# One ring of seven eviction buffers, mask and rotary-key operand laid over it, rotary query rows first: a hybrid attention layer on one Trainium2 core

## The chip, the cores and the metric

The program runs on one core of a Trainium2 chip. The metric is the device time of one launch in microseconds (us); lower is better. Engines are named as the profile names them: PE (TensorE matmuls), PEld (its weight loads), DVE (VectorE), ACT (ScalarE), POOL (GpSimd) and SP (SyncE, which here only issues DMAs).

## The reference

One layer of a hybrid encoder over 1072 rows: 32 sample rows, 16 meta rows and 1024 prompt rows, with a cache of 512 older rows for the sample stream. Cut to what matters here:

```python
c_q, c_kv, k_r, f_q, f_k, f_v, f_logit = jnp.split(h @ w_in, IN_SPLIT_POINTS, axis=-1)
q = (rms_norm(c_q, q_norm) @ w_uq).reshape(B, L, MLA_HEADS, MLA_QK_DIM)
q_mla = jnp.concatenate([q[..., :MLA_NOPE], rope(q[..., MLA_NOPE:], pos)], axis=-1)
latent = rms_norm(c_kv, kv_norm)
k_rope = rope(k_r[:, :, None, :], pos)[:, :, 0, :]
kv = (latent @ w_ukv).reshape(B, K, MLA_HEADS, MLA_NOPE + MLA_V)   # MLA keys, values
o_a = attend(q_mla, k_mla, v_mla, MLA_SCALE, chunk mask)           # 8 heads
o_b = attend(f_q, f_k, f_v, FOX_SCALE, causal, fox_bias(cum, cum)) # 8 forgetting heads
x = x + jnp.concatenate([o_a, o_b], -1) @ w_out
h = rms_norm(x, norm_ffn)
return x + (jax.nn.silu(h @ w_gate) * (h @ w_up)) @ w_down
```

## The kernel before, in words

Every float32 operand of a product is kept as a rounded high part and a low part, and a product is three matmuls (high by high, high by low, low by high: `mm3`, lines 119 to 121). The function `split` makes the two parts: ACT copies the high one, DVE (or POOL for some weights) subtracts. `spill` and `spill_v` split a PSUM result into an eviction buffer in SBUF and send it to a scratch tensor in DRAM with a DMA that POOL issues (`put`, line 63). `load` and `move` are DMAs that SP issues (lines 57 and 60).

The program has three stages. The first normalizes the input and makes the projections (PE's lines 291 to 384). The second is attention, in two halves: heads 8 to 15 (forgetting) and then heads 0 to 7 (latent). `attention` walks the heads; `fetch` and `fetch_v` load the operands of the next head; `scores` multiplies (line 579), finds the row maximum on DVE (line 582) and takes the exponential on ACT (line 587); `values` transposes (lines 617, 641), splits and multiplies with the values (lines 627, 655 to 658). The third stage is the output projection's second half and the feed-forward network (line 805 on).

Between the pieces of attention a *filler* is stepped, so that PE has other products to do. For heads 8 to 15 the filler is `latent_heads(ev)`: 16 steps that make the latent keys (`w_uk`, four blocks by four column chunks, to `sK`), 26 steps that make the latent values (`w_uv`, line 485 on, to `sV`), and 18 steps that make the queries (`w_uq`, blocks m = 0 to 5 by three chunks; m 0 to 3 go to `sQ`, m 4 and 5 are the rotary rows and go to `sQR`). For heads 0 to 7 the filler is `out_half(ev)`: 24 half products of the output projection with a residual read from `xT` and a result sent to `sX2`. All filler products share one PSUM buffer, the tile `psF`.

The eviction buffers before: key and query steps use two tiles `es` of the pool `evq` and, every third step, a free part of the slot `A_lo` (function `es(n)`, lines 458 to 463). Value steps use two parts of the slot `A_hi` (`vts`, line 465). A rotary step loads its factors into the one tile `cs` (line 508), with the one temporary `et` and one `et2`. `out_half` has two tiles `xt`.

The tile `B3` holds three copies of the rotary keys and ten rows of masks. Heads 0 to 7 multiply with it in `scores`; its four moves (lines 764 to 767) stand in the code ahead of the first attention half.

The order on each engine is made by the framework from the code when the program is built; each engine then works strictly in that order. Buffers are guarded by semaphores: whoever writes a buffer waits for all who used it, so an eviction into a buffer waits until the DMA out of it has landed.

Of the kernel before, what the change touches and what calls it, by code (L numbers as in the profile page):

```python
# [9 lines left out]
F32 = mybir.dt.float32  # L10
# [30 lines left out]
FC = [(0, 408), (408, 408), (816, 256)]  # L41
LAG = 2
LN_EXP = "natural_log_exp_and_others"
OB = 112
# [4 lines left out]
def trunk(ctx: ExitStack, tc: tile.TileContext, a):  # L49
# [6 lines left out]
    def load(out, in_):  # L56
        sp.dma_start(out=out, in_=in_)
# [383 lines left out]

    def latent_heads(ev):

# [12 lines left out]
        turn = [0]  # L456

        def es(n):

            turn[0] += 1  # L460
            if turn[0] % 3 == 0:
                return lo[:, 3 * T:3 * T + 2 * n].rearrange("p (j t) -> p j t", j=2)
            return ev.tile([128, 2, 396], FR, tag="es", name="es")

        vts = [hi[:, 3 * T + 512 * j:3 * T + 512 * j + 512].rearrange("p (h d) -> p h d", h=4) for j in range(2)]
        todo = [("w_uk", m, 2, 128) for m in range(4)] + [("w_uv", m, 2, 256) for m in range(2)]
        ws = [weights(*todo[0])]
        yield
        for m in range(6):
            if m + 1 < 6:  # L470
                ws.append(weights(*todo[m + 1]))
            w = ws[m]
            if m < 4:
                for c0, n in KC:
                    ps = psF.tile([128, 512], F32, tag="psF", name="psF")
                    mm3(ps[:, :n], lambda k: w[0][:, k], lambda k: w[1][:, k],
                        lambda k: l_hi[:, k, c0:c0 + n], lambda k: l_lo[:, k, c0:c0 + n], 2)
                    spill(es, sK[m, :, :, c0:c0 + n], ps[:, :n], n)
                    yield
            else:  # L480
                for kt, (k0, n) in enumerate([(128 * i, 128) for i in range(4)] + [(PAST + t0, n) for t0, n in QT]):
                    ps = psF.tile([128, 512], F32, tag="psF", name="psF")
                    for k in range(2):
                        s_hi, s_lo = l_hi[:, k, k0:k0 + 128], l_lo[:, k, k0:k0 + 128]
                        pe.matmul(ps[:, :256], s_hi, w[0][:, k], start=(k == 0), stop=False)
                        pe.matmul(ps[:, :256], s_hi, w[1][:, k], start=False, stop=False)
                        pe.matmul(ps[:, :256], s_lo, w[0][:, k], start=False, stop=(k == 1))
                    spill_v(ev, k0, 4 * (m - 4), ps[:n, :256], n, vts[kt % 2])
                    yield
# [3 lines left out]
        move(c_lo, sCQ[:, :, 1].rearrange("k p t -> p k t"))  # L493
        ws = [weights("w_uq", 0, 3, 128)]
        yield
        for m in range(6):
            if m + 1 < 6:
                ws.append(weights("w_uq", m + 1, 3, 128))
            w = ws[m]
            for c0, n in CC:  # L500
                ps = psF.tile([128, 512], F32, tag="psF", name="psF")
# [4 lines left out]
                else:  # L506
                    cs = ev.tile([128, 2, 358], F32, tag="cs", name="cs", bufs=1)
                    load(cs[:, :, :n], a["trig"][:, :, c0:c0 + n])
                    t1 = ev.tile([128, 358], F32, tag="et", name="et", bufs=1)
                    act.activation(t1[:, :n], ps[:, :n], AF.Copy, scale=SCALE)  # L510
                    t2 = ev.tile([128, 358], F32, tag="et2", name="et2", bufs=1)
                    dve.stream_shuffle(t2[:, :n], t1[:, :n], [(i + 16) % 32 for i in range(32)])
                    dve.tensor_tensor(out=t2[:, :n], in0=t2[:, :n], in1=cs[:, 1, :n], op=ALU.mult)
                    dve.tensor_tensor(out=t1[:, :n], in0=t1[:, :n], in1=cs[:, 0, :n], op=ALU.mult)
                    dve.tensor_tensor(out=t1[:, :n], in0=t1[:, :n], in1=t2[:, :n], op=ALU.add)
                    spill(es, sQR[m - 4, :, :, c0:c0 + n], t1[:, :n], n)
                yield

# [9 lines left out]

    def out_half(ev):

        hi, lo = (rows4(t) for t in mixed["B"])
        out_weights(1)
        for m in range(8):
            out_weights(m + 2)
            w = w_ring[m]
            for c0, n in CC:
                xt = ev.tile([128, 358], F32, tag="xt", name="xt")
                load(xt[:, :n], a["xT"][128 * m:128 * m + 128, c0:c0 + n])
# [176 lines left out]
    def attention(hs, filler, steps, last):  # L715
# [11 lines left out]
        for h in hs:  # L727
# [4 lines left out]
            if h == hs[-1]:  # L732
                for _ in filler:
                    pass
            nops = fetch(nxt) if nxt in heads else None
            if h % 2 == 0:
# [26 lines left out]
    mixed["B"] = (slot("B_hi"), slot("B_lo"))  # L763
    B3 = st.tile([106, NK], FR, tag="B3", name="B3", bufs=1)
    for j, part in enumerate((0, 0, 1)):
        move(B3[32 * j:32 * j + 32], sKR[:, part])
    move(B3[96:106], sMK[0:10])
    mixed["B3"] = B3
    with tc.tile_pool(name="evq", bufs=2) as ev:
        attention(range(8, 16), latent_heads(ev), 62, False)  # L770
    mixed["A"] = (slot("A_hi"), slot("A_lo"))
    with tc.tile_pool(name="evo", bufs=2) as ev:

        attention(range(0, 8), out_half(ev), 48, True)
        for _ in state["pend"]:
            pass
    B.close()
# [282 lines left out]
```

## Time and profile before

| what | value |
|---|---|
| median of 3 runs | 1563.72 us (1559.86 to 1563.76) |
| the profiled execution's own time | 1564.27 us |
| span of its instructions | 1562.5 us |
| PE busy | 1502.2 us (96%) |
| DVE busy | 969.3 us (62%) |
| ACT busy | 594.3 us (38%) |
| POOL busy | 213.4 us (14%) |
| mean granted TensorE clock | 0.987 |
| first attention half, then second, in the trace | about 233 to 488 us, about 488 to 711 us |

The profiled execution lies 0.55 us above the median of the runs, and 1.8 us of its time lie outside the span. A share of busy time is an average over the three stages, so it does not say which engine sets the end in attention. Matmuls are pipelined and their ends are modelled in the trace, so PE counts as busy for a little while after it has stopped.

### The profile page before, as it was taken

What the parts mean: (1) busy time and instruction counts of PE and PEld (TensorE: products, weight loads), DVE (VectorE), ACT (ScalarE), POOL (GpSimd) and SP (SyncE); (2) the same over time, 40 slices, a digit from 0 to 9 for tenths busy, and PEclk for the clock granted to TensorE, in tenths of its full rate; (3) what the DMA queues carried; (4) which work ended last, traced back from release to release, by engine and by line L of the source; (5) the groups of instructions that cost most, each with busy time, mean ns of one, the idle gap of its engine ahead of it and who ended that gap; (6) DMA issues with size and microseconds to landing.
All of it is one profiled execution on the core that took longest, in us unless ns stands there. A gap on an engine that the chain in (4) does not pass through costs nothing.

```text
span 1562.5 us, 24281 instructions
## 1 busy us (share of the span) xinstructions
PE 1502.2 (96%) x9309; PEld 1440.7 (92%) x9309; DVE 969.3 (62%) x1853; ACT 594.3 (38%) x1204; POOL 213.4 (14%) x342
## 2 busy tenths in 40 slices
PE   9999998988998999999999999999999999999995
PEld 8999997877787988888999999999999999999995
DVE  7874616756767666775945556555555555555647
ACT  7453436655765665663611111111112111111124
POOL 0343241422232122210000000000000000000014
PEclk9999999999999999999999999999999999999998
DMA  5689557766867767625101111111111111111003
GB/s 193 234 256 307 168 199 214 254 176 183 234 202 194 198 163 181 161 70 193 55 28 41 61 54 49 42 41 41 41 41 41 47 63 54 41 41 41 28 1 113
DMA packets 88469, 185.28 MB, mean 119 GB/s; under 512 B 9819, under 2 KB 53787, under 8 KB 88261
## 3 DMA queue, kind: packets, MB, share of 16 engines
q1 hardware_dynamic: 71424, 129.44, 28.7%
q0 software_dynamic: 16928, 54.29, 9.9%
q8 instruction: 74, 1.21, 0.3%
q14 instruction: 43, 0.34, 0.1%
HBM read 125.02 MB, written 58.67 MB: 118 GB/s over the span
## 4 chain that ended last, share of the span: by engine, by line
PE 82%; DMA 5%; DVE 4%; ACT 4%; issue 3%; POOL 1%; SPq 0%; DVEq 0%; POOLq 0%; ACTq 0%
PE psG L120 11%; PE psG L119 11%; PE psG L121 11%; PE psD L873 5%; PE psD L874 5%; PE psD L872 5%; PE psS L579 4%; PE psA L121 3%; PE psA L119 3%; PE psA L120 3%; PE psT L641 3%; PE po L657 2%; DMA sV<-A_hi 2%; PE po L658 1%; DMA sK<-es 1%
## 5 line engine op out<-in xcount | busy, mean ns | idle before, releaser
L881 DVE TENSOR_TENSOR x<-psD,x 128x408 f32<-128x408 f32 (+1 forms) x496 | 236.3, 522 | 5.7 <-PE psD L874 5.7
L119 PE MATMUL psG<-B_hi,gh 128*128 128x408 f32 (+1 forms) x528 | 172.7, 327 | 0.0
L119 PE MATMUL psG<-A_hi,gh 128*128 128x408 f32 (+1 forms) x528 | 172.6, 327 | 0.0
L120 PE MATMUL psG<-A_lo,gh 128*128 128x408 f32 (+1 forms) x528 | 172.6, 327 | 0.0
L120 PE MATMUL psG<-B_lo,gh 128*128 128x408 f32 (+1 forms) x528 | 172.5, 327 | 0.0
L874 PE MATMUL psD<-ah,dl 128*128 128x408 f32 (+1 forms) x528 | 172.1, 326 | 0.0
L121 PE MATMUL psG<-B_hi,gl 128*128 128x408 f32 (+1 forms) x528 | 171.8, 325 | 0.0
L121 PE MATMUL psG<-A_hi,gl 128*128 128x408 f32 (+1 forms) x528 | 171.8, 325 | 0.0
L873 PE MATMUL psD<-al,dh 128*128 128x408 f32 (+1 forms) x528 | 171.7, 325 | 0.0
L872 PE MATMUL psD<-ah,dh 128*128 128x408 f32 (+1 forms) x528 | 170.9, 325 | 0.1
L861 ACT ACTIVATE sl<-sl 128x408 f32<-128x408 f32 (+1 forms) x66 | 33.1, 502 | 354.4 <-DVE sl L860 354.4
L865 DVE TENSOR_TENSOR sq<-psG,rb 128x408 f32<-128x408 f32 (+1 forms) x66 | 34.9, 529 | 155.9 <-PE psG L121 155.9
L812 POOL TENSOR_TENSOR acc<-acc,sq 128x408 f32<-128x408 f32 x14 | 15.0, 1069 | 810.7 <-ACT sq L811 810.0
L67 DVE TENSOR_TENSOR ptl<-psT,pth 128x512 fp32r<-128x512 f32 x192 | 104.1, 552 | 31.1 <-ACT pth L66 29.0
L582 DVE TENSOR_REDUCE nm<-psS 128x1 f32<-128x656 f32 (+2 forms) x144 | 104.1, 725 | 30.1 <-PE psS L579 28.6
L66 ACT ACTIVATE pth<-psT 128x512 fp32r<-128x512 f32 (+4 forms) x208 | 98.6, 480 | 56.6 <-PE psT L641 48.2
L579 PE MATMUL psS<-b,a 128*128 128x328 f32 (+4 forms) x360 | 103.3, 338 | 9.3 <-ACT pb L587 5.5
L860 DVE TENSOR_TENSOR sl<-psG,rb 128x408 f32<-128x408 f32 (+1 forms) x66 | 34.9, 529 | 123.3 <-PE psG L121 123.3
L66 ACT ACTIVATE ah<-sl 128x408 fp32r<-128x408 f32 (+1 forms) x66 | 33.2, 503 | 192.3 <-DVE sl L866 121.3
L120 PEld LDWEIGHTS psG<-A_lo,gh 128*128 128x128 f32 x528 | 99.3, 188 | 0.5 <-issue 0.3
L872 PEld LDWEIGHTS psD<-ah,dh 128*128 128x128 f32 x528 | 99.2, 188 | 0.5 <-ACT ah L66 0.3
L119 PEld LDWEIGHTS psG<-A_hi,gh 128*128 128x128 f32 x528 | 99.2, 188 | 0.5 <-issue 0.2
(276 smaller groups left out, 3830.2 us busy)
## 6 DMA issues: line engine op xcount, KB each, us to landing
sg<-w_gu SPq DMA_DIRECT2D x44, 512.0 KB
a<-sQ SPq DMA_DIRECT2D x56, 268.0 KB
b<-sK SPq DMA_DIRECT2D x32, 396.0 KB
sg<-w_down SPq DMA_DIRECT2D x22, 512.0 KB
v<-sV SPq DMA_DIRECT2D x16, 512.0 KB
wst<-w_in SPq DMA_DIRECT2D x13, 512.0 KB
sV<-vt POOLq DMA_DIRECT2D x24, 256.0 KB, 3.8
sV<-A_hi POOLq DMA_DIRECT2D x24, 256.0 KB, 3.7
```

The costliest lines, as they stand in the source:

```text
L66: act.activation(hi, src, AF.Copy)
L67: eng.tensor_tensor(out=lo, in0=src, in1=f32(hi), op=ALU.subtract)
L119: pe.matmul(ps, whi(k), rhi(k), start=(k == 0), stop=False)
L120: pe.matmul(ps, whi(k), rlo(k), start=False, stop=False)
L121: pe.matmul(ps, wlo(k), rhi(k), start=False, stop=(k == K - 1))
L579: pe.matmul(out, qa[:K, t0:t0 + nq], kb[:K, k0 + c:k0 + c + w], start=(j == 0), stop=last)
L582: dve.tensor_reduce(out=nm[:nq, j:j + 1], in_=src, axis=AX.XY if len(src.shape) == 3 else AX.X, op=ALU.max, negate=True)
L641: pe.transpose(out=pt[:, 128 * g:128 * g + 128], in_=tiles[g][1][:, c:c + 128], identity=ident)
L872: pe.matmul(ps, dh[:, m], ah[:, cs], start=first and j == 0, stop=False)
L873: pe.matmul(ps, dh[:, m], al[:, cs], start=False, stop=False)
L874: pe.matmul(ps, dl[:, m], ah[:, cs], start=False, stop=last and j == len(parts) - 1)
L881: dve.tensor_tensor(out=x2[:, m, cs], in0=ps[:, :n], in1=x2[:, m, cs], op=ALU.add)
```

## The change

The pools `evq` and `evo` go. Three tiles `room0` to `room2` of 128 x 1584 take their place, each cut in two, so there are six parts (`ring`), and the free part of `A_lo` is the seventh. All evictions of `latent_heads`, keys, values and queries, go round these seven. The rotary blocks m = 4 and 5 are made first of the six query blocks. Their factors are loaded once, three chunks into ring parts 0 to 2, and the temporaries lie in part 3; during these six steps the evictions go round parts 4, 5 and the part of `A_lo`. `out_half` uses parts 0 to 3 as eight half buffers. The rotary-key and mask operand is laid over `room2` (parts 4 and 5), and its four moves are made by `masks()` when the first filler has come to its end, at head 15.

```diff
+RING = 6
-    def latent_heads(ev):
+    def latent_heads():
...
+        def part():
+            turn[0] = (turn[0] + 1) % (RING + 1)
+            return ring[turn[0]] if turn[0] < RING else lo[:, 3 * T:3 * T + 792]
         def es(n):
-            turn[0] += 1
-            if turn[0] % 3 == 0:
-                return lo[:, 3 * T:3 * T + 2 * n].rearrange("p (j t) -> p j t", j=2)
-            return ev.tile([128, 2, 396], FR, tag="es", name="es")
-        vts = [hi[:, 3 * T + 512 * j:3 * T + 512 * j + 512].rearrange("p (h d) -> p h d", h=4) for j in range(2)]
+            return part()[:, :2 * n].rearrange("p (j t) -> p j t", j=2)
...
-                    spill_v(ev, k0, 4 * (m - 4), ps[:n, :256], n, vts[kt % 2])
+                    spill_v(None, k0, 4 * (m - 4), ps[:n, :256], n, part()[:, :512].rearrange("p (h d) -> p h d", h=4))
...
-        ws = [weights("w_uq", 0, 3, 128)]
+        trig = [f32(ring[i][:, :716].rearrange("p (j t) -> p j t", j=2)) for i in range(3)]
+        for t, (c0, n) in zip(trig, CC):
+            load(t[:, :, :n], a["trig"][:, :, c0:c0 + n])
+        order = (4, 5, 0, 1, 2, 3)
+        ws = [weights("w_uq", order[0], 3, 128)]
...
-                    cs = ev.tile([128, 2, 358], F32, tag="cs", name="cs", bufs=1)
-                    load(cs[:, :, :n], a["trig"][:, :, c0:c0 + n])
-                    t1 = ev.tile([128, 358], F32, tag="et", name="et", bufs=1)
+                    turn[0] = max(turn[0], 3)
+                    t1, t2 = (f32(ring[3][:, 358 * j:358 * j + 358]) for j in range(2))
                     act.activation(t1[:, :n], ps[:, :n], AF.Copy, scale=SCALE)
-                    t2 = ev.tile([128, 358], F32, tag="et2", name="et2", bufs=1)
...
                     spill(es, sQR[m - 4, :, :, c0:c0 + n], t1[:, :n], n)
+                    if turn[0] == RING:
+                        turn[0] = 3
...
-    def out_half(ev):
+    def out_half():
...
-                xt = ev.tile([128, 358], F32, tag="xt", name="xt")
+                turn = (turn + 1) % 8
+                xt = f32(ring[turn // 2][:, 396 * (turn % 2):396 * (turn % 2) + 358])
...
             if h == hs[-1]:
                 for _ in filler:
                     pass
+                if not last:
+                    masks()
...
-    B3 = st.tile([106, NK], FR, tag="B3", name="B3", bufs=1)
-    for j, part in enumerate((0, 0, 1)):
-        move(B3[32 * j:32 * j + 32], sKR[:, part])
-    move(B3[96:106], sMK[0:10])
-    mixed["B3"] = B3
-    with tc.tile_pool(name="evq", bufs=2) as ev:
-        attention(range(8, 16), latent_heads(ev), 62, False)
+    rooms = [st.tile([128, 2 * 792], FR, tag=f"room{i}", name=f"room{i}", bufs=1) for i in range(RING // 2)]
+    ring = [rooms[i // 2][:, 792 * (i % 2):792 * (i % 2) + 792] for i in range(RING)]
+    def masks():
+        B3 = rooms[-1][:106]
+        for j, part in enumerate((0, 0, 1)):
+            move(B3[32 * j:32 * j + 32], sKR[:, part])
+        move(B3[96:106], sMK[0:10])
+        mixed["B3"] = B3
+    attention(range(8, 16), latent_heads(), 62, False)
```

The change also moves instructions. Lines after the first are one higher in the changed file up to line 450, and up to 14 higher behind that.

**PE where the first filler step stands** (head 8 to 9; psS are scores, psT transposes, po the products with the values, psF the filler). Before, the stretch just ahead of the first filler step:

```order
L579 MATMUL psS<-b_2606,a_2603 128x456
L578 LDWEIGHTS identb
L578 MATMUL psS<-trib,identb 128x128
L579 MATMUL psS<-x,a_2609 128x456
L641 MATMUL psT<-ident,pa 128x128
L579 MATMUL psS<-b_2606,a_2603 128x346
L579 MATMUL psS<-x,a_2609 128x346
L119 MATMUL psF<-A_hi,woh 128x396
```

With the change, where a_2546 is still head 8's query operand:

```order
L586 LDWEIGHTS identb
L586 MATMUL psS<-trib,identb 128x128
L587 MATMUL psS<-x,a_2546 128x264
L649 MATMUL psT<-ident,pb 128x128 x3
L120 MATMUL psF<-A_hi,woh 128x396
L121 MATMUL psF<-A_lo,woh 128x396
L122 MATMUL psF<-A_hi,wol 128x396
```

The first filler step moved from the scores of head 9 to the later scores of head 8, some 50 rows of this list forward. From the eighth value step on, the filler steps stand at the same places among the attention products as before.

**SP at the start of attention** (sL are the latent rows, sKR the rotary keys, sM the masks). Before:

```order
L60 DMA A_hi<-sL 128x2x396
L60 DMA A_lo<-sL 128x2x396
L60 DMA B_2595<-sKR 32x1584 x3
L60 DMA B_2595<-sM 10x1584
L60 DMA A_hi<-sL 128x2x396
L60 DMA A_lo<-sL 128x2x396
```

With the change, from the last of the latent rows on:

```order
L61 DMA A_hi<-sL 128x2x396
L61 DMA A_lo<-sL 128x2x396
L58 DMA wst<-w_uk 128x256 x4
L61 DMA a_2878<-sQ 64x1072 x2
L61 DMA b_2881<-sK 64x1584 x2
```

The four moves of the rotary keys and masks are gone from among the latent rows, and four weight loads follow at once.

**SP between the two attention halves**, with the change (a_5326 and b_5329 are head 0's operands, a_5602 and b_5605 head 1's; room_2597 is `room2`):

```order
L58 DMA wst<-w_uq 128x384 x2
L61 DMA b_5329<-sK 64x1584 x2
L61 DMA x<-sQR 32x1072 x3
L61 DMA a_5326<-sQ 64x1072 x2
...
L58 DMA wst<-w_out 128x512
L61 DMA a_5602<-sQ 64x1072 x2
L61 DMA b_5605<-sK 64x1584
L61 DMA room_2597<-sKR 32x1584 x3
L61 DMA room_2597<-sM 10x1584
L61 DMA b_5605<-sK 64x1584
```

The moves of the rotary keys and masks now stand behind the first loads for head 1, whose first operand becomes free when head 15's last score is done. The six loads `cs<-trig` that stood in this stretch before are gone; three such loads stand earlier, one ahead of head 14's operands and two behind the load of `sCQ`.

## Rows read from the trace of the kernel before

**Rows 1.** The page's first line, engine table and granted clock in 40 slices.
```profile
span 1562.5 us, 24281 instructions
PE 1502.2 (96%) x9309; PEld 1440.7 (92%) x9309; DVE 969.3 (62%) x1853; ACT 594.3 (38%) x1204; POOL 213.4 (14%) x342
PEclk9999999999999999999999999999999999999998
```

**Rows 2.** Windows: length, busy us (instructions) of each engine, granted clock, DMA share, GB/s.
```profile
core 0: us, PE busy (x) PEld busy (x) DVE busy (x) ACT busy (x) POOL busy (x), PEclk, DMA share, GB/s
232.00:260.00 28.00, 23.60 (x132) 18.54 (x131) 17.32 (x29) 17.42 (x42) 3.57 (x8) 0.91 0.66 205
260.00:300.00 40.00, 37.60 (x229) 33.04 (x227) 26.01 (x50) 24.96 (x60) 13.39 (x23) 0.98 0.85 259
300.00:400.00 100.00, 84.64 (x563) 74.11 (x561) 65.13 (x136) 62.40 (x160) 28.22 (x50) 0.95 0.62 178
400.00:460.00 60.00, 58.06 (x375) 51.40 (x375) 41.42 (x82) 39.26 (x96) 17.47 (x28) 1.00 0.79 230
460.00:500.00 40.00, 34.38 (x192) 29.10 (x191) 33.37 (x71) 24.07 (x59) 12.81 (x20) 0.92 0.85 235
500.00:700.00 200.00, 192.84 (x1251) 175.47 (x1249) 139.41 (x265) 123.39 (x294) 36.50 (x65) 1.00 0.59 152
720.00:1540.00 820.00, 819.23 (x4987) 815.98 (x4985) 479.48 (x925) 182.12 (x287) 14.96 (x14) 1.00 0.14 47
```

**Rows 3.** Waits of PE, 232 to 520 us: total, times, longest.
```profile
PE psF L485 <- DVE A_hi L67: 10.7, 6, 4.1
PE psF L119 <- DVE es L67: 2.3, 4, 1.0
PE po L657 <- ACT pth L66: 2.0, 1, 2.0
```

**Rows 4.** Waits of ACT, 232 to 520 us.
```profile
ACT A_hi L66 <- DMA sV<-A_hi: 19.6, 8, 4.9
ACT es L66 <- DMA sK<-es: 2.9, 2, 1.9
ACT A_lo L66 <- DMA sK<-A_lo: 0.5, 1, 0.5
```

**Rows 5.** Timeline about one stall: start us, length us, engine, work [idle before it, and what ended it].
```profile
328.53 0.38 ACT L66 ACTIVATE A_hi<-psF 128x256 fp32r<-128x256 f32 x1 [4.88 <-DMA sV<-A_hi]
328.95 0.43 DVE L67 TENSOR_TENSOR A_hi<-psF,A_hi 128x256 fp32r<-128x256 f32 x1 [4.54 <-ACT A_hi L66]
329.43 0.39 PE L485 MATMUL psF<-woh,A_hi 128*128 128x256 f32 x1 [4.12 <-DVE A_hi L67]
329.67 0.54 POOL L63 DMA_DIRECT2D sV<-A_hi  x1 [5.91 <-DVE A_hi L67]
```

**Rows 6.** Tile A_hi, 300 to 400 us: min/median/max ns, first and last start; its DMAs' landing.
```profile
L66 ACT ACTIVATE A_hi<-psF x26: 373/383/388, 307.7 to 393.5; 128x256 fp32r<-128x256 f32 x24, 48x256 fp32r<-48x256 f32 x2
...
DMA to landing us min/median/max: 2.1/3.7/8.3
```

**Rows 7.** Chain that ended last, 232 to 262 us: start, length, what.
```profile
233.86 6.39 DMA B<-sKR
240.32 8.46 DMA wst<-w_uk
248.82 8.52 issue
```

**Rows 8.** Timeline of SP, PE, POOL and PE at the start of attention.
```profile
232.99 1.30 SPq L60 DMA_DIRECT2D B<-sKR  x3
...
245.96 0.37 PE L579 MATMUL psS<-x,a 70*128 70x264 f32 x1
...
257.38 1.42 POOL L67 TENSOR_TENSOR wol<-wst,woh 128x256 fp32r<-128x256 f32 x2 [22.17 <-ACT woh L66]
...
257.47 0.35 PE L119 MATMUL psF<-A_hi,woh 128*128 128x396 f32 x1
```

**Rows 9.** Waits of DVE, 232 to 520 us, then 500 to 715 us.
```profile
DVE et L513 <- DMA cs<-trig: 1.9, 2, 1.3
...
DVE xt L546 <- DMA xt<-xT: 0.9, 1, 0.9
```

**Rows 10.** Timeline of PE: head 15's last score, then the first product with B3.
```profile
465.69 0.38 PE L579 MATMUL psS<-x,a 70*128 70x280 f32 x1
488.59 0.39 PE L579 MATMUL psS<-B,x 106*128 106x328 f32 x1
```

**Rows 11.** Landing of the DMAs that tile es takes part in, whole span.
```profile
DMA to landing us min/median/max: 2.8/4.7/10.8
```

**Rows 12.** Timeline of SP, 426 to 446 us.
```profile
427.49 16.71 SPq L57 DMA_DIRECT2D wst<-w_uq  x2
```

More of the change, by code (lines that the diff above doesn't have):

```diff
@@ L480, in latent_heads @@
             else:
-                for kt, (k0, n) in enumerate([(128 * i, 128) for i in range(4)] + [(PAST + t0, n) for t0, n in QT]):
+                for k0, n in [(128 * i, 128) for i in range(4)] + [(PAST + t0, n) for t0, n in QT]:
                     ps = psF.tile([128, 512], F32, tag="psF", name="psF")
@@ L493, in latent_heads @@
         move(c_lo, sCQ[:, :, 1].rearrange("k p t -> p k t"))
-        ws = [weights("w_uq", 0, 3, 128)]
-        yield
[L496 to L500, printed above, removed]
+        trig = [f32(ring[i][:, :716].rearrange("p (j t) -> p j t", j=2)) for i in range(3)]
[3 more added lines that the diff above has]
+        ws = [weights("w_uq", order[0], 3, 128)]
+        yield
+        for i, m in enumerate(order):
+            if i + 1 < 6:
+                ws.append(weights("w_uq", order[i + 1], 3, 128))
+            w = ws[i]
+            for cs, (c0, n) in zip(trig, CC):
                 ps = psF.tile([128, 512], F32, tag="psF", name="psF")
@@ L527, in out_weights @@
             w_next[0] += 1
-    def out_half(ev):
+    def out_half():
         hi, lo = (rows4(t) for t in mixed["B"])
+        turn = 0
         out_weights(1)
@@ L763, in trunk @@
     mixed["B"] = (slot("B_hi"), slot("B_lo"))
-    B3 = st.tile([106, NK], FR, tag="B3", name="B3", bufs=1)
-    for j, part in enumerate((0, 0, 1)):
-        move(B3[32 * j:32 * j + 32], sKR[:, part])
-    move(B3[96:106], sMK[0:10])
-    mixed["B3"] = B3
-    with tc.tile_pool(name="evq", bufs=2) as ev:
-        attention(range(8, 16), latent_heads(ev), 62, False)
+    rooms = [st.tile([128, 2 * 792], FR, tag=f"room{i}", name=f"room{i}", bufs=1) for i in range(RING // 2)]
[7 more added lines that the diff above has]
+    attention(range(8, 16), latent_heads(), 62, False)
     mixed["A"] = (slot("A_hi"), slot("A_lo"))
[L772 to L776, printed above, removed]
+    attention(range(0, 8), out_half(), 48, True)
+    for _ in state["pend"]:
+        pass
     B.close()
```

## The prediction

> **What bounds the kernel now.** Three views were read in this order. The page says that PE is busy 96% of the span at almost full clock [rows 1], so time can only be won where PE is idle or slowed. The windows by stage [rows 2] say where that is. In the feed-forward network PE is idle 0.8 us of 820; nothing is to be won there. In the second attention half, 500 to 700 us, it is idle 200 - 192.84 = 7.2 us, 3.6%, at full clock; in 400 to 460 us it is 1.9 us of 60, 3.2%. Take 3.5% as what attention with a filler costs anyway. Against that the first half stands out: 4.4 us idle in 232 to 260, 2.4 in 260 to 300, 15.4 in 300 to 400, 5.6 in 460 to 500. Less 3.5% of each stretch, this leaves 3.4, 1.0, 11.9 and 4.2 us, together 20.5 us. In the same stretches the granted clock is 0.91, 0.98, 0.95 and 0.92: a part of them runs at 1.2 GHz instead of 2.4. The missing share times the length is 2.5, 0.8, 5.0 and 3.2 us, together 11.5 us of full-speed time.
>
> The waits then say what PE waits for. Its longest item is the value product's PSUM buffer, 10.7 us in six waits [rows 3], and behind that stands ACT, which waits 19.6 us in eight places for a `sV` DMA to leave an eviction buffer [rows 4]. One such stall reads as a chain [rows 5]: ACT may write `A_hi` only when the DMA has landed (4.88 us idle), DVE follows, then PE (4.12 us idle), then POOL issues the next DMA. All four engines stand still. A landing takes up to 8.3 us [rows 6], a value step comes about every 3.4 us (26 evictions between 307.7 and 393.5 us [rows 6]), so two buffers cover 6.8 us and not 8.3; seven cover 24.
>
> **The change part by part**, against the profiled execution of 1564.3 us.
>
> *Value evictions, two buffers to seven.* The wait for the landing goes: at 24 us of cover no landing shown reaches it. The gain is between 8.3 us (the part of PE's idle time that comes back if this stretch keeps 7% idle, as POOL and ACT still work in order) and 19.6 us (all that ACT waits). I take the excess of 11.9 us: it lies beside the 10.7 + 2.0 us that PE's own waits show [rows 3]; the second is PE behind an ACT that waits, and PE's clock of idleness is what the end sees.
>
> *Key evictions, three buffers to seven.* ACT waits 2.9 + 0.5 us here [rows 4], PE 2.3 us [rows 3], the excess is 1.0 us. Between 1.0 and 3.4 I take 1.0, the row of the stretch.
>
> *The start.* SP's four moves of the rotary keys no longer stand among the latent rows. In the chain they land after 6.39 us, the first filler weights land 8.46 us after their issue, and then POOL still waits until 257.4 us, since ACT's copies of the weights stand behind 8.5 us of other work [rows 7, 8]. With the change the loads carry 0.67 MB less (by the shapes, three times 32 x 1584 and ten rows more, at 4 bytes). At the 205 GB/s of this stretch [rows 2] the weights land some 3 us sooner, at about 246 us. The order now has the first filler step right behind the score that PE ran at 245.96 us, where it ran at 257.47 before [rows 8]. PE cannot win more than its idle time and lost clock there, 4.4 + 2.5 us; if the weights land late, PE stalls and loses up to 1 us. I take 2.5 us of idleness. The two further weight loads that now stand ahead of head 10's operands on SP make these wait for two POOL splits, 1.42 us [rows 8]; a head takes some 30 us (eight in 255), so this costs nothing.
>
> *The rotary rows first.* The six loads of factors go, and with them DVE's waits of 1.9 us [rows 9]; the three that remain stand on SP ahead of or with the `sCQ` rows, which the query steps wait for anyway. DVE does the same work but no longer in one lump: it is busy 33.4 of 40 us in 460 to 500 against 41.4 of 60 in 400 to 460 [rows 2]. PE's excess there is 4.2 us; not all comes back, since the first scores of head 0 still wait for an operand that comes late. Between -1 (the lump only moves) and 4.2 I take 2.5.
>
> *Rotary keys and masks over room 2.* This adds a wait. The moves start when the query evictions of parts 4 and 5 have landed, and head 0 needs them. From head 15's last score to the first product with `B3` PE has 22.9 us of work and waits now [rows 10], 18.7 without the excess of 4.2 just counted. The chain in that time is: eviction and issue about 2 (0.38, 0.43 and 0.54 [rows 5], and some queueing), landing 4.7 (up to 10.8) [rows 11], four issues 1.7 (1.30 for three) [rows 8], landing 6.4 [rows 7], so 15 to 21 us. Behind the moves on SP stand the rest of head 1's operands, due a head later, 28 us (eight heads in 223). Cost 0 to 8 us (2.3 of overrun, and 6 more if SP comes late by a landing); I take 1, since the median landing lies near the low end.
>
> *Residual reads.* Eight half buffers for two: DVE's one wait of 0.9 us [rows 9] goes; 0.5.
>
> *The clock.* The 11.5 us of lost clock lie in the stretches whose waits go. Not each drop needs a long wait, and PE is not always what is waited for, so between 0 and 11.5 I take half, 5.8. Weighed against the rule: in 500 to 700 us the filler also has a single PSUM buffer and the clock is 1.00 [rows 2]. The Trainium skill, in TensorE: Matmul & The Clock Gate, section A second HAM failure mode: psum-queue depth-cycling, speaks against this gain: a kernel that cycles through its PSUM queue idles shortly between groups often enough for the clock to swing without any long wait. By that rule the drops stay and the sum loses its 5.8 us; by the row they go with the waits.
>
> Sum: 11.9 + 1.0 + 2.5 + 2.5 - 1 + 0.5 + 5.8 = 23.2 us. 1564.3 - 23.2 = 1541.1. The median of the runs is 0.55 us under the profiled execution, so **1541 us** for the median of the changed kernel, give or take. All upper ends together would be 45 us, all lower ends nothing; they do not come together. The forecast's own range is 1530 to 1550.
>
> **Rivals.** About 0.3% (4.7 us) is what a measurement of this kernel can tell from no change.
>
> *The clock drops stay*, from the short pauses at the one filler buffer. Against it: the clock of 1.00 with the same single buffer in the second half. For it: in 460 to 500 us the clock is 0.92, and DVE's longest wait for factors is 1.3 us [rows 9]. 1541 + 5.8 = 1547 us. The page of the Trainium skill named under the clock would have this case the likely one.
>
> *DVE becomes the bound.* Its 65.1 us in 300 to 400 would have to fit in 84 us, 78% busy. At 65% (260 to 300) PE is idle 6%, at 83% (460 to 500) 14% [rows 2]; between them some 10%, so 8.6 us of the value stretch stay idle instead of 3. That is 5.6 us less, and no clock comes back: 1541 + 5.6 + 5.8 = 1552 us. Against it: part of the DVE work in 460 to 500 waits rather than works.
>
> *The ring does not do what it says*, because the DMA engines and not the buffers are the limit: then a deeper ring only makes landings longer. For it: a DMA share of 0.85 in 260 to 300. Against it: 0.62 where the stalls are [rows 2]. Start, rotary rows and reads alone less the new wait: 1564 - 4 = 1560 us.
>
> *Slower: SP comes late to the mask moves.* SP works in order, and two weight loads in this stretch held it for 16.71 us before [rows 12]. With the change, a pair of `w_uq` loads stands right ahead of head 0's operands and a `w_out` load right ahead of head 1's and the mask moves. If each held SP so long, 33.4 us plus 1.7 and 6.4 make 41.5 against the 18.7 us that PE can cover: PE stands 22.8 us, and some 5 us of the clock and rotary gain go too. 1541 + 28 = 1569 us. It decides from the point where the moves are issued over 34 us after head 15's last score (18.7 of cover + 23.2 of gain less 8.1 of issue and landing). Against it: those weight buffers come free at query steps well ahead of that score.
>
> **How the numbers follow.** The forecast has 0.62, the clock 0.12, DVE 0.13, the ring 0.05, SP 0.08. Faster by over 0.3% (under 1559) are the first three, 0.87; within it the ring case, 0.05; slower 0.08. The range reaches past the DVE case and leaves out the last two and the ends of the forecast's own: 1529 to 1556 us.
>
> **What would show it.** In the windows of the new profile, 300 to 385 us should have PE idle under 5%, at a clock of 0.98 or more; ACT should have no wait for a `sV` DMA; the first filler step should stand near 247 us; DVE should have no wait for factors. The mask moves should be issued within 12 us of head 15's last score, and PE's wait ahead of its first product with room 2 should be under 3 us. The feed-forward network should take the same time to within 2 us. The prediction is wrong if PE's idle time only moves to other releasers, DVE or ACT, in the same windows, or if a new wait of over 5 us stands between the two halves.

## The result and the profile after

| kernel | median us (lowest to highest, runs) | ratio to the kernel before, 95% interval |
|---|---|---|
| before, same chip | 1562.85 (1559.86 to 1563.76, 4) | 1 |
| changed | 1541.82 (1541.08 to 1544.53, 4) | 0.9873, 0.9859 to 0.9888 |

The change saves 21.0 us; 1541 was forecast. The execution behind the profile is the longest of the four, 1544.53 us.

The page's first line, engine table (here PE) and granted clock, which answer to [rows 1]:

```profile
span 1542.8 us, 24296 instructions
PE 1494.8 (97%) x9309; PEld 1435.6 (93%) x9309; DVE 972.7 (63%) x1853; ACT 595.6 (39%) x1204; POOL 212.8 (14%) x342
PEclk9999999999998999999999999999999999999998
```

The windows by stage, with the columns of [rows 2]. Their borders move with the work, which now runs ahead:

```profile
232.00:260.00 28.00, 24.70 (x140) 20.19 (x139) 17.01 (x30) 17.26 (x43) 7.41 (x13) 0.94 0.74 246
260.00:300.00 40.00, 39.23 (x250) 34.03 (x249) 30.76 (x60) 29.48 (x70) 14.45 (x24) 1.00 0.76 241
300.00:385.00 85.00, 82.76 (x593) 73.02 (x591) 68.01 (x140) 65.26 (x167) 24.68 (x49) 1.00 0.82 242
385.00:440.00 55.00, 46.41 (x283) 40.13 (x283) 46.92 (x92) 34.07 (x82) 13.64 (x19) 0.97 0.59 159
440.00:480.00 40.00, 36.59 (x209) 31.98 (x207) 21.96 (x43) 19.36 (x45) 12.86 (x22) 0.91 0.97 251
480.00:680.00 200.00, 194.53 (x1259) 177.30 (x1260) 141.08 (x268) 127.32 (x305) 37.65 (x66) 0.99 0.59 152
700.00:1520.00 820.00, 819.23 (x4987) 816.02 (x4986) 479.58 (x925) 182.16 (x287) 15.00 (x14) 1.00 0.15 47
```

The value stretch, 300 to 385 us, has come right: PE is idle 2.24 us of 85 (2.6%, against 15.4 of 100 in [rows 2]) at full clock. The feed-forward network is the same. The stretch behind the values has got worse, though: from 385 to 440 us, where the rotary steps now stand, PE is idle 8.6 us of 55, while DVE is 85% busy. Up to 480 us it is idle 12.0 us of 95, where the kernel before has 7.5 of 100 (400 to 500 us in [rows 2]).

The longest waits of PE and then of ACT from 300 to 385 us (who waits, for whom; total, times, longest), for [rows 3, 4]:

```profile
PE psT L625 <- DVE ptm L654: 0.8, 1, 0.8
```

```profile
ACT pth L67 <- PE psT L649: 6.6, 15, 0.8
ACT room L67 <- PE psF L488: 3.7, 5, 1.1
```

ACT, PE and DVE wait for no value store (`sV<-`) any more. ACT now waits for PE, as it should when PE sets the pace.

PE's last score of head 15, SP's issue of the mask moves and PE's first product with room 2 (start, length, what), for [rows 8, 10]:

```profile
452.68 0.38 PE L587 MATMUL psS<-x,a 70*128 70x280 f32 x1
```

```profile
460.65 1.57 SPq L61 DMA_DIRECT2D room<-sKR  x3
```

```profile
470.75 0.40 PE L587 MATMUL psS<-room,x 106*128 106x328 f32 x1
```

The moves leave 8.0 us after that score and 10.1 us ahead of the product, which waits for nothing.

### The profile page after: what moved, and what is told of

Same layout as the page of the kernel before. It is cut to its first block, busy times and chain, and to the rows that moved or that the text cites. A ratio compares the mean times of both kernels' runs of the same rounds, so it can differ in the third digit from the quotient of the medians.

```text
span 1542.8 us, 24296 instructions
## 1 busy us (share of the span) xinstructions
PE 1494.8 (97%) x9309; PEld 1435.6 (93%) x9309; DVE 972.7 (63%) x1853; ACT 595.6 (39%) x1204; POOL 212.8 (14%) x342
## 4 chain that ended last, share of the span: by engine, by line
PE 88%; DVE 5%; ACT 3%; issue 2%; DMA 1%; POOL 0%; DVEq 0%; SPq 0%; ACTq 0%; POOLq 0%
PE psG L121 11%; PE psG L120 11%; PE psG L122 11%; PE psD L887 5%; PE psD L888 5%; PE psD L886 5%; PE psS L587 5%; PE psT L649 5%; PE psA L122 3%; PE psA L120 3%; PE psA L121 3%; PE po L665 2%; PE po L666 2%; PE psA L384 1%; PE psA L385 1%
```

## The experiments

My theory after the trace: the value ring is nearly all of the gain. The rivals: the earlier start of the filler, the clock alone, or the order of the rotary rows. The kernel before ran beside each group on the same chip, and the ratios are to it; its medians were 1563.83 us (e1 to e4), 1561.86 (e5 to e8), 1563.07 (e9, e10) and 1563.28 (e11, e12).

| run | median us (lowest to highest) | ratio, 95% interval |
|---|---|---|
| e1 changed, value steps on 2 parts | 1561.13 (1558.48 to 1564.21) | 0.9981, 0.9971 to 0.9992 |
| e2 before, value steps on 5 parts | 1545.47 (1544.59 to 1549.35) | 0.9883, 0.9868 to 0.9899 |
| e3 changed, rotary rows last | 1542.21 (1540.71 to 1542.66) | 0.9856, 0.9842 to 0.9869 |
| e4 changed, B3 in its own tile | 1542.83 (1541.48 to 1544.30) | 0.9862, 0.9848 to 0.9875 |
| e5 changed, value steps on 3 parts | 1544.00 (1541.88 to 1547.06) | 0.9889, 0.9873 to 0.9904 |
| e6 changed, value steps on 4 parts | 1545.19 (1540.82 to 1545.79) | 0.9885, 0.9868 to 0.9902 |
| e7 rotary and query steps alternate | 1554.03 (1552.71 to 1556.89) | 0.9956, 0.9940 to 0.9972 |
| e8 rotary products on GpSimd | 1549.72 (1548.82 to 1551.65) | 0.9925, 0.9912 to 0.9938 |
| e9 own buffer for the small spread | 1543.55 (1542.18 to 1546.88) | 0.9883, 0.9863 to 0.9902 |
| e10 alternating, 4 parts, spread's buffer | 1539.05 (1537.80 to 1540.20) | 0.9853, 0.9835 to 0.9871 |
| e11 changed kernel again | 1543.46 (1541.31 to 1545.28) | 0.9866, 0.9843 to 0.9889 |
| e12 as e10, without the spread's buffer | 1538.78 (1538.20 to 1539.03) | 0.9840, 0.9818 to 0.9862 |

**e1 and e2: the value ring taken out alone, and put in alone.** In e1 the value steps of the changed kernel are back to two parts:

```diff
...
-    spill_v(None, k0, 4 * (m - 4), ps[:n, :256], n, part()[:, :512]...)
+    spill_v(None, k0, 4 * (m - 4), ps[:n, :256], n, ring[kt % 2][:, :512]...)
```

> The changed kernel, its value steps alone confined to two parts of the ring (key and query steps keep all of it). Theory (the waits of value evictions for their own stores were most of the gain): 1554 to 1560 us, ACT waits behind sV stores for over 10 us again, and half-speed stretches come back between 300 and 400 us. Rival A (the gain came from the earlier start of the filler and from the masks' later place): 1541 to 1546 us. Rival B (only TensorE's clock mattered, and it follows the queue of its PSUM buffer, not the evictions): 1541 to 1546 us with the same clock row as the changed kernel.

In e2 the kernel before takes its two `vts`, the tail of `A_lo` and its two `es` tiles in turn for values, and nothing else is changed:

```diff
-        vts = [hi[:, 3 * T + 512 * j:3 * T + 512 * j + 512]... for j in range(2)]
+        def vts(j):
+            if j < 2:
+                t = hi[:, 3 * T + 512 * j:3 * T + 512 * j + 512]
+            elif j == 2:
+                t = lo[:, 3 * T:3 * T + 512]
+            else:
+                t = ev.tile([128, 2, 396], FR, tag="es", name="es")...[:, :512]
...
-                    spill_v(ev, k0, 4 * (m - 4), ps[:n, :256], n, vts[kt % 2])
+                    spill_v(ev, k0, 4 * (m - 4), ps[:n, :256], n, vts(kt % 5))
```

> The kernel before, its value steps alone spread over five buffers that it already holds (two in A_hi, one in A_lo, the two of es); everything else as before. Theory: 1546 to 1550 us, by 13 to 17 us under the kernel before, since the trace of the change gave about 17 us up to the first product with B3. Rival A (start and masks): 1558 to 1563 us.

On its chip e1 lies only 2.7 us under the kernel before (1563.83 - 1561.13), so it loses 18.3 of the 21.0 us; e2 alone wins 18.4 (1563.83 - 1545.47). Both lie up to 1.1 us outside the range that my theory gave them, on the side of a larger gain from the ring. The two agree: about 18 us are the value ring, and all else together is 2 to 3 us. The trace of e1 has the stall back. Below are its waits of ACT, then of PE, 232 to 520 us, and its window from 300 to 400 us:

```profile
ACT room L67 <- DMA sV<-room: 19.1, 7, 4.7
```

```profile
PE psF L486 <- DVE room L68: 10.4, 6, 3.1
```

```profile
300.00:400.00 100.00, 85.22 (x571) 75.06 (x571) 66.52 (x138) 63.89 (x166) 24.70 (x47) 0.95 0.68 203
```

These are close to the numbers of the kernel before: 19.6 us of ACT and 10.7 us of PE [rows 3, 4], 84.64 us busy, clock 0.95 [rows 2]. The same window of e2:

```profile
300.00:400.00 100.00, 95.85 (x676) 84.02 (x674) 79.36 (x161) 75.59 (x191) 29.00 (x54) 1.00 0.81 235
```

PE's idle time there falls from 15.4 to 4.2 us and the lost clock from 5.0 us to nothing. Rivals A and B fall: e1 keeps the early start, the masks' late place and the single PSUM buffer of the filler, and has the slow time. That the clock follows the stall is shown; how the 18.4 us divide between stall and clock is worked out only. The two windows give 11.2 us of idle time and 5.0 us of clock, 16.2 together; PE's waits of 10.7 + 2.0 us [rows 3] and the clock's 5.0 us make 17.7.

**e5 and e6: how deep must the ring be?** The edit is that of e1 with `kt % 3` and `kt % 4`.

> The changed kernel with its value steps confined to three parts of the ring. A value store of 10.8 us lands over a step every 3.8 us or so: with two parts 19.3 us came back. If each wait is what is left of the store's time after the steps between (a linear cover), a third part takes away one step's length of each of some 24 waits and nearly all of them go: 1543 to 1548 us. If the stores queue behind each other on the way to memory (a throughput limit that more parts only postpone), half or more of the 19 us stays: 1549 to 1556 us.

> The same with four parts. Linear cover: 1541 to 1543 us, the same as seven parts. Throughput limit: between the run with three parts and the changed kernel, 1545 us or more.

Both lie within each other's scatter, 2.2 and 3.4 us above the changed kernel's first median and 0.5 and 1.7 above its second (e11), with overlapping intervals. On its chip e5 saves 17.9 us (1561.86 - 1544.00) where e1 saved 2.7 on another, so the third part brings about 15 of the 18 us. (The 10.8 us in the expectation of e5 are the longest landing of tile `es` [rows 11]; that of a value store was 8.3 us [rows 6].) e6 stands a little above its bound of 1543 us and at that of the rival; but between its trace and that of e5 the waits do what a linear cover says. Waits of ACT, 232 to 520 us, of e5 and then of e6:

```profile
ACT room L67 <- DMA sV<-room: 5.3, 3, 2.5
```

```profile
ACT room L67 <- DMA sV<-room: 2.1, 1, 2.1
```

From two parts to seven they go 19.1, 5.3, 2.1, none. The longest landing of a ring part from 300 to 385 us hardly moves, 8.2 us in e1 and 8.5 in the changed kernel, though the median goes from 3.4 to 4.9. So the DMA engines were not the limit. What parts five to seven bring is too small for these runs to tell from nothing.

**e3: the rotary rows last again.**

```diff
-        order = (4, 5, 0, 1, 2, 3)
+        order = (0, 1, 2, 3, 4, 5)
+        turn[0] = max(turn[0], 3)
...
-                    turn[0] = max(turn[0], 3)
...
-                    if turn[0] == RING:
-                        turn[0] = 3
+                if turn[0] == RING:
+                    turn[0] = 3
                 yield
```

> The changed kernel with the order of the query weights put back (0 to 5, rotary rows last); its factors are still loaded once. My term for making them first was a gain of 2.5 us (bounds a loss of 1 to a gain of 4.2), so by it 1544 us. Theory after the trace of the change (VectorE is full from 385 to 440 us whichever comes first there, and PE's idle time of 8.6 us in that stretch is its price): 1539 to 1543 us, no gain from the order. Rival (the order keeps the rotary rows out of the way of head 15, and is the larger part of what came before 471 us): 1547 us or more, with waits of head 0's fetch for sQR.

The time is the same: 1542.21 us, 21.6 under the kernel before on its chip. In e3 the factors lie in the ring through all query steps, so that all their evictions go round three parts; but in its trace ACT waits for none of these stores. Its windows show why the time is the same; 385 to 440 us first, then 440 to 480:

```profile
385.00:440.00 55.00, 52.72 (x330) 45.26 (x329) 37.41 (x74) 35.21 (x86) 16.19 (x24) 1.00 0.71 197
440.00:480.00 40.00, 31.64 (x162) 25.70 (x161) 29.46 (x62) 18.65 (x43) 11.60 (x19) 0.87 0.84 223
```

PE's idle time is 2.3 and 8.4 us here, where the changed kernel has 8.6 and 3.4. The lump goes where the rotary steps go, and its price with it.

**e4: the masks and rotary keys in a tile of their own, filled at the start.** The ring keeps four parts and takes the tail of `A_hi` beside that of `A_lo`.

```diff
-RING = 6
+RING = 4
...
-            turn[0] = (turn[0] + 1) % (RING + 1)
-            return ring[turn[0]] if turn[0] < RING else lo[:, 3 * T:3 * T + 792]
+            turn[0] = (turn[0] + 1) % (RING + 2)
+            return ring[turn[0]] if turn[0] < RING else (hi, lo)[turn[0] - RING][:, 3 * T:3 * T + 792]
...
-                    if turn[0] == RING:
+                    if turn[0] == RING + 1:
...
-                if not last:
-                    masks()
...
+    B3 = st.tile([106, NK], FR, tag="B3", name="B3", bufs=1)
...
-        B3 = rooms[-1][:106]
...
+    masks()
     attention(range(8, 16), latent_heads(), 62, False)
```

> The changed kernel with B3 in a tile of its own, filled ahead of the latents as before; the ring keeps four of its six parts and takes the tail of A_hi beside that of A_lo (six parts in all). Theory (SP is kept from the latents' moves by B3's four): first filler product near 249 us instead of 245.9, and 1543 to 1547 us, of which the masks' return to the start gives back at most 1 us between the halves. Rival (the filler is only a list of dues, so its start matters nothing): 1540 to 1543 us.

The filler's first product is 11 us later, more than I expected. Tile psF, 232 to 262 us, of the changed kernel and then of e4 (durations min/median/max, then first and last start):

```profile
L120 PE MATMUL psF<-A_hi,woh x12: 339/346/449, 245.9 to 259.6; 128*128 128x396 f32 x12
```

```profile
L120 PE MATMUL psF<-A_hi,woh x4: 338/346/446, 257.0 to 260.6; 128*128 128x396 f32 x4
```

The time is nevertheless the same, as the rival had it: e4 saves 21.0 us on its chip, as the changed kernel did on its own. The clock of the two traces differs, too. The window 232 to 500 us of the changed kernel, then of e4:

```profile
232.00:500.00 268.00, 249.04 (x1579) 216.89 (x1578) 198.10 (x385) 178.95 (x436) 75.38 (x129) 0.97 0.76 217
```

```profile
232.00:500.00 268.00, 246.89 (x1592) 215.14 (x1592) 198.21 (x387) 179.18 (x438) 75.66 (x129) 0.99 0.77 224
```

This trace of e4 has 2% more clock over 268 us, some 5 us, but its execution was also the shorter one, 1541.48 against 1544.53 us. Over all four executions of each kernel the mean granted clock lies between 0.989 and 0.992 in both. Where the drops behind the value stretch fall also differs between executions of one kernel: the changed kernel has 0.97 and 0.91 in 385 to 440 and 440 to 480 us, and run again (e11) 0.94 and 0.99. So this difference is none of the edit's. What the overlay and the late masks bring as a whole, though, is measured: nothing that can be told from zero.

**e7, e8, e9: the lump of rotary work.** Two theories of what it costs: DVE's load as such, or single collisions with GpSimd. One collision stands in the changed kernel at 403.7 us. DVE, GpSimd (POOL) and PE in the timeline (start, length, what, idle before it):

```profile
398.26 0.52 DVE L519 TENSOR_TENSOR room<-room 128x358 f32<-128x358 f32 x1
...
403.74 2.75 DVE L519 TENSOR_TENSOR room<-room 128x358 f32<-128x358 f32 x1
```

```profile
403.51 0.41 POOL L423 CAST v<-zeros 128x128 fp32r<-128x128 f32 x1
403.77 1.38 POOL L713 TENSOR_TENSOR B_lo<-raw,B_hi 128x512 fp32r<-128x512 f32 x1
405.01 1.09 POOL L68 TENSOR_TENSOR wol<-wst,woh 128x384 fp32r<-128x384 f32 x1
```

```profile
406.66 1.76 PE L649 MATMUL psT<-ident,pb 128*128 128x128 f32 x7 [2.03 <-DVE raw L710]
```

The same add that takes 0.52 us in the step before is not done until the last two operations of GpSimd are, and PE waits 2.03 us for what DVE does next. e7 alternates the steps (4 with 0, 5 with 1, then 2 and 3; weights come two steps ahead in place of three):

```diff
-        order = (4, 5, 0, 1, 2, 3)
+        steps = [(m, c) for c in range(3) for m in (4, 0)] + [(m, c) for c in range(3) for m in (5, 1)]
+        steps += [(m, c) for m in (2, 3) for c in range(3)]
+        nxt = {4: 5, 5: 1, 10: 2, 11: 3}
...
-        for i, m in enumerate(order):
+        for i, (m, c) in enumerate(steps):
```

> The changed kernel with rotary and query steps alternating (4 with 0, then 5 with 1, then 2 and 3), so VectorE's rotary work is spread over 12 steps. If PE's idle time of 8.6 us from 385 to 440 us (2.4 us of it in the run with the rotary rows last, which lost 8.4 us from 440 to 480 instead) is the price of their density, 5 to 7 us go: 1535 to 1538 us. If it is the price of single collisions that any order meets (one rotary add took 2.75 us beside two operations of GpSimd back to back), 1540 to 1543 us.

Neither came: e7 is 12 us slower than the changed kernel. Its trace has two holes. First PE and ACT in the one, then PE in the other, with SP's issue of the masks' moves:

```profile
443.88 0.67 PE L120 MATMUL psF<-A_hi,woh 128*128 128x356 f32 x1 [6.13 <-DVE room L142]
```

```profile
442.79 0.47 ACT L141 ACTIVATE room<-psF 128x358 fp32r<-128x358 f32 x1 [6.36 <-DMA sQR<-room]
```

```profile
479.88 0.61 PE L592 MATMUL psS<-room,x 106*128 106x328 f32 x1 [5.18 <-DMA room<-sM]
```

```profile
473.82 1.30 SPq L61 DMA_DIRECT2D room<-sKR  x3
```

While the factors lie in the ring, evictions have three parts, and now query steps used them too; one had to wait for a rotary row's store. And SP issued the masks' moves over room 2 only at 473.82 us (460.65 in the changed kernel), too late for head 0. That is the slower rival of the prediction in small, though through the last stores out of room 2 (SP waits 9.9 us for one) and not through weight loads.

e8 moves three operations of each rotary step:

```diff
-                    dve.tensor_tensor(out=t2[:, :n], in0=t2[:, :n], in1=cs[:, 1, :n], op=ALU.mult)
-                    dve.tensor_tensor(out=t1[:, :n], in0=t1[:, :n], in1=cs[:, 0, :n], op=ALU.mult)
-                    dve.tensor_tensor(out=t1[:, :n], in0=t1[:, :n], in1=t2[:, :n], op=ALU.add)
+                    pool.tensor_tensor(out=t2[:, :n], in0=t2[:, :n], in1=cs[:, 1, :n], op=ALU.mult)
+                    pool.tensor_tensor(out=t1[:, :n], in0=t1[:, :n], in1=cs[:, 0, :n], op=ALU.mult)
+                    pool.tensor_tensor(out=t1[:, :n], in0=t1[:, :n], in1=t2[:, :n], op=ALU.add)
```

> The changed kernel with the two products and the sum of each rotary step on GpSimd in place of VectorE (the shuffle stays). It takes 18 times 0.52 us, 9.4 us, off VectorE and puts 18 operations of about 0.95 us, 17 us, on GpSimd, which is about 14 us busy of those 55. If VectorE's load as such makes PE idle there: 1536 to 1539 us. If what hurts is VectorE held up while GpSimd works on the same memory side (operations with all operands in SBUF took 1.2 to 2.75 us there beside GpSimd, 0.52 alone), GpSimd's longer work brings as many such collisions with what stays on VectorE: 1540 to 1545 us.

1549.72 us is above both. The window 385 to 440 us of e8, one of the products (385 to 440 us), and two waits, of ACT and of PE, 385 to 480 us:

```profile
385.00:440.00 55.00, 45.83 (x254) 40.03 (x255) 31.58 (x64) 29.31 (x71) 29.45 (x37) 0.91 0.51 143
```

```profile
L517 POOL TENSOR_TENSOR room<-room,room 128x358 f32<-128x358 f32 x4 | 3.9, 975 | 1.9 <-DVE room L516 1.9
```

```profile
ACT room L67 <- POOL room L519: 7.8, 4, 3.1
```

```profile
PE psS L587 <- ACT pa L595: 2.7, 1, 2.7
```

DVE's load falls from 46.92 to 31.58 us of 55, and PE is idle 9.2 us instead of 8.6, at a lower clock. So less load on DVE alone brought nothing. Whether the load was the limit before, e8 does not show, since a longer chain took its place: a product takes 0.98 us here for 0.52, and ACT, which works in order, sits before the rounding copy of the rotary row with the exponentials queued behind it.

e9 gives the third spread of a pair's reciprocals a buffer of its own, since GpSimd sat 12.8 us before it, and I took it that stores were queued behind:

```diff
-            bc = st.tile([128, 4, 2, 64], F32, tag="bc", name="bc")
+            bc = st.tile([128, len(ts_), 2, 64], F32, tag=f"bc{len(ts_)}", name="bc", bufs=2 if len(ts_) > 1 else 1)
```

> The changed kernel, where the third and small spread of each pair's reciprocals gets a buffer of its own, so that GpSimd no longer sits up to 12.8 us before it with the eviction stores queued behind. In the changed kernel nobody on PE waited for a store, so if the ring of seven already covers these delayed stores: 1540 to 1543 us, no change. If the delays still reach PE through the parts: 1535 to 1539 us.

No change: 1543.55 us, and 1543.46 for the changed kernel on the same chip (e11). The trace shows that nothing could come of it. The wait is gone, but in its place GpSimd waits 14.53 us for ACT (line 711), and the next store in its queue, of the first rotary row, leaves at 403.13 us, 402.91 in the changed kernel. No store had stood behind that wait alone.

**e10 to e12: e7 with its two holes mended.** e10 is e7 plus the edit of e9, a further part, and the last steps off room 2:

```diff
-            turn[0] = (turn[0] + 1) % (RING + 1)
-            return ring[turn[0]] if turn[0] < RING else lo[:, 3 * T:3 * T + 792]
+            turn[0] = (turn[0] + 1) % (RING + 2)
+            return ring[turn[0]] if turn[0] < RING else (lo, hi)[turn[0] - RING][:, 3 * T:3 * T + 792]
...
             if i < 11:
                 turn[0] = max(turn[0], 3)
+            elif turn[0] == 3 or turn[0] == 4:
+                turn[0] = RING - 1
...
-            if i < 11 and turn[0] == RING:
-                turn[0] = 3
+            if turn[0] == RING + 1:
+                turn[0] = 3 if i < 11 else -1
```

> The run with rotary and query steps alternating lost 12 us on the changed kernel, in two holes of 6.1 and 5.2 us (an eviction behind a rotary row's store, and B3's masks behind the last stores of room 2). Here the small spread has its own buffer as in the run beside it, evictions have four parts in place of three while the factors lie in the ring (the tail of A_hi), and the last six steps keep off room 2. If late stores made the 12 us: 1541 us or less, and 1536 to 1538 if density of VectorE's rotary work is the rest of the idle time there. If the alternation itself is what costs (weights fetched two steps ahead in place of three): 1548 us or more, with PE waits for woh or wol before the query steps.

e12 is e10 without the edit of e9, and e11 is the changed kernel beside it.

> The alternating order with four eviction parts and the last steps off room 2, but without the small spread's own buffer, which moved nothing when it stood alone. If parts and order give the 3 us under the changed kernel: 1537 to 1541 us, and 2 to 4 us under the run beside it. If the spread's buffer was needed here, since GpSimd's 12.8 us wait falls on the first rotary stores: 1544 us or more.

> The changed kernel once more, on the same chip as the run beside it: 1541 to 1544 us.

e10's 1539.05 us is under the 1541 that late stores alone would leave, but above the 1536 to 1538 that the spread was to bring. e12 beats both kernels: 1538.78 us, every run under every run of e11, whose median is 4.7 us higher. The late stores made e7's loss, since the alternation is the same. Windows 385 to 440 and 440 to 480 us of e11, then of e12:

```profile
385.00:440.00 55.00, 46.32 (x274) 40.04 (x273) 46.25 (x91) 33.51 (x81) 13.61 (x19) 0.94 0.59 159
440.00:480.00 40.00, 35.51 (x218) 31.27 (x216) 22.55 (x44) 20.26 (x46) 12.90 (x23) 0.99 0.95 252
```

```profile
385.00:440.00 55.00, 49.16 (x308) 41.60 (x307) 47.10 (x97) 36.33 (x89) 14.69 (x20) 1.00 0.67 177
440.00:480.00 40.00, 37.66 (x239) 33.21 (x238) 27.88 (x53) 24.89 (x61) 11.11 (x21) 1.00 0.81 236
```

PE's idle time falls from 8.7 to 5.8 and from 4.5 to 2.3 us, 5.0 us together, at a clock of 1.00 in both, though DVE is busier than in e11. PE's wait of 2.0 us behind the collision, which e11 has too, is not in e12's trace. How much of it is the spread of the rotary steps and how much the earlier release of room 2 (its moves are issued at 439.01 us, 461.99 in e11) was not tried apart.

## Why the prediction was right, and where its steps were not

**Value evictions.** The mechanism was right in each link: two buffers cover less than a landing, ACT waits, PE stands behind it, and the ring takes it away. The size was too small. The prediction took 11.9 us of idle time and half of the clock's 5.0 us in this stretch, 14.4 together; 18.4 (e2) and 18.3 (e1) were measured. The idle time was about right, 11.2 us by the windows of e2. What went wrong is that the clock was put into a term of its own and halved, though the 5.0 us of this stretch hang on the same stall and came back whole. Some 2 us are left over, which is within the interval of e2. Two details of the working were off. The 3.4 us a step contain the stalls: in e5 the 26 value stores leave every 3.0 us. And the cover must hold the eviction and the issue as well as the landing: by the prediction's rule three parts (10.2 us) would outlast every landing of 8.3 us, but e5 has three waits left. The lower bound of 8.3 us should be 8.4 (15.4 less 7.0); nothing hangs on it.

**The clock** as a whole, 5.8 us. In the value stretch it did come back, 0.95 to 1.00. Elsewhere drops stay (0.97 from 385 to 440 us and 0.91 from 440 to 480; 0.94 and 0.99 in e11). Over whole executions the mean granted clock is 0.9865 in the kernel before beside e1 to e4 (14 executions) and 0.990 in the changed kernel (four); times the span that is some 6 us, an estimate. So the term was about right as a sum, and wrong in taking half of every stretch. The rival "the clock drops stay" from the one PSUM buffer of the filler is refuted for the value stretch: e1 and e2 both keep that buffer, and the clock is 0.95 with the stall and 1.00 without it. By the rule in the Trainium skill, TensorE: Matmul & The Clock Gate, section A second HAM failure mode: psum-queue depth-cycling, the drops would have stayed in e2 too; no run here shows it at work in that stretch.

**The start**, 2.5 us. The filler's first product came at 245.9 us, as worked out, but e4 puts it back to 257.0 us, with the masks early and one ring part fewer, and saves the same 21.0 us. The step that failed is "PE cannot win more than its idle time and lost clock there", which was then taken for a win: the window 232 to 260 us did gain 1.1 us of PE work, 24.70 against 23.60 [rows 2], but the end did not move. My reading, which no run shows, is that a filler works off a fixed amount, and work done earlier only counts if PE would otherwise end later.

**The rotary rows first**, 2.5 us, bounds -1 to 4.2. Measured by e3: nothing. "The lump only moves", the reading behind the lower bound, was the truth. The sign that I gave for being wrong, idle time that moves to other releasers in the same windows, is there in 385 to 440 us. The rival "DVE becomes the bound" did not come where it was looked for: in the value stretch DVE is 80% busy and PE idle 2.6%. Something near it came in the 55 us from 385 to 440, where I had not looked. What makes PE idle there is shown in part: 2.0 of the 8.6 us stand behind one DVE operation that GpSimd held up. It is not DVE's load alone, since e12 has DVE busier and PE idle 2.8 us less.

**Key evictions, masks, residual reads**, 1.0, -1 and 0.5 us, were not taken apart. ACT's waits for `sK` [rows 4] and DVE's for `xT` [rows 9] are gone from the trace (ACT has one of 1.2 us for a `sQR` store), and the new wait for the masks never reached PE. With the start and the rotary rows these make the 2 to 3 us that e1 and e2 leave; which of them brings it stays open.

**The sum.** That 1541 was hit so closely is in part luck, since errors cancel: the value ring with the clock of its stretch gave about 18.4 us, where 14.4 were forecast, and start and rotary rows gave about nothing where 5.0 were. The saving was forecast at 23.2 us and came to 21.0.

**The ring** and **SP late** did not come. e5 and e6 rule out the first. The second decides by when room 2 is free, as e7 shows: there PE waited 5.18 us for the masks.

## What to carry to other kernels

When an eviction waits for its own store, count parts against the longest landing and add one: here 8.3 us over 3.0 us a step make three and one more, the third buffer brought about 15 of 18 us, and the rest of the ring could hardly be measured. Price such a stall by its idle time and all of the clock lost in that stretch, not half. A lump of work that is moved takes its price along; spread it, and check which buffers its spreading keeps busy.

## What the runs showed of the hardware

An operation of DVE with all operands in SBUF can be held while GpSimd works on SBUF: one took 2.75 us at 403.74 us instead of 0.52. GpSimd was in a cast from 403.51 us, and two more of its operations followed without a gap, the second of them 1.3 us after DVE's start. In e11 it is the same, 2.75 us at 403.69. A second case in the changed kernel, GpSimd and then DVE:

```profile
424.08 1.01 POOL L68 TENSOR_TENSOR wol<-wst,woh 128x384 fp32r<-128x384 f32 x1 [0.17 <-ACT woh L67]
```

```profile
424.22 1.26 DVE L517 TENSOR_TENSOR room<-room 128x356 f32<-128x356 f32 x1
```

In both cases of the changed kernel DVE ends 0.39 us after GpSimd does. The time in which it is held counts as DVE busy. I had priced DVE's work by its own durations and GpSimd's (14% busy) at nothing.

The Trainium skill states the cause in SBUF — State Buffer, section SBUF: two separate sides: DVE and GpSimd share a pair of ports as an exclusive lock, and a DVE operation with two SBUF inputs contends for it with a GpSimd operation that reads SBUF. The trace agrees that DVE blocks fully. The page also says that whoever starts first gets the pair for the whole instruction. The trace agrees in that GpSimd had begun before DVE both times (403.51 and 424.08 us); that DVE then stood behind two further operations of GpSimd, recorded at 403.77 and 405.01 us, the sentence does not cover.
